# Two margins instead of one in the planner of a hybrid decoder trunk

## The chip, the cores and the metric

The kernel runs on one core of one Trainium2 chip. The metric is the device time of one execution in microseconds (us). Three executions of the kernel before took 1103.56, 1106.44 and 1106.52 us; the median is 1106.44 us.

## The reference

The program is one inference step of a two-layer decoder trunk in fp32 (D_MODEL 2048, a prompt of 256 tokens and 8 sample tokens, so 264 columns). Cut to what matters:

```
h = rms_norm(x, norm_w)
z = h @ w_in                      # 2048 x 7296, columns split among branches
y_a = rwkv_time_mix(z_a, ...)     # 12 heads x 64: decay, delta-rule state scan, group norm, gate
y_b = attention_branch(z_b, ...)  # 3 dilated windows, 12 heads; samples read KV caches of 2048
y_c = pool_branch(z_c, ...)       # causal means over 2, 4, 8, 16 rows, a 128x128 map per group
y = x + concat([y_a, y_b, y_c]) @ w_out   # 2048 x 2048
```

Each layer also returns the updated states and the new K/V rows. The state scan of the prompt is computed in chunks of 64 tokens: triangular systems are inverted by blocks, and four chunks follow one another through small products.

## The kernel before, in words

**The stream.** TensorE's main work is the two large projections, called the stream here. Weights arrive as 512 KB tiles `raw` over SyncE's queue (SP); `stream` (line 323 holds its matmul) splits each into a rounded part `hi` (ScalarE, line 137) and a remainder `lo` (VectorE, line 140) and multiplies hi by the two parts of x and lo by the first part: for one `raw` tile of two 128-column halves, 24 matmuls of 128x128 by 264 columns. Over both layers that are 5472 matmuls against w_in and 1536 against w_out, 7008 in all, into three PSUM banks with the tag `acc`. The order of the column tiles is fixed by the program; w_out takes its rows in quarters in the order 2, 1, 3, 0, so its first matmul needs the attention outputs in the tiles `mb`.

**The side products.** Everything else on TensorE, 2794 instructions, writes the five banks with the tag `a` and is called a side product: transposes (line 118), the rank-64 maps, the blocks of the inversion (`invert`), the chunk products (`chunk`), scores and values of the attention (`b_prompt`), the samples' products over the caches (`b_sample`, with the tiles `vc`, `ex`, `os`), and the pooling maps (`cd`). Some are tied into bundles that stay together. Each reads what ScalarE, VectorE, GpSimd or a transfer has just written, and its result goes back to ScalarE or VectorE. TensorE runs its instructions strictly in the order in which they are written, so a side product whose operand is late holds up the stream matmuls behind it.

**The planner.** The program is first written out branch by branch; then `Plan` puts all instructions of all engines into a new order. `Plan.once` is a list scheduler that simulates the engines with costs per instruction (`cost`, line 1467 on), hop times between engines (`HOP`) and DMA times. An instruction becomes ready when its operands are done in this simulation, plus a hop, plus the instruction's `slack`. Stream matmuls, and instructions that feed them (`hi`, `lo`), have slack 0; all others have `margin`, 350 ns. The slack counts only for operands from another engine or from a transfer:

```
slack = [0 if stream[k] or k in feeds else margin for k in range(n)]
...
r = fin[k] if dma[k] else fin[k] + (100 if eng[q] == "SP" else HOP[e, eng[q]])
if e != eng[q] or dma[k]:
    r += slack[q]
```

On TensorE a ready side product goes before any stream matmul; the stream fills the rest. On the other engines the ready instruction with the longest remaining chain goes first. The plan is made twice: the first pass gives the start times from which non-weight loads are held back (`ahead`, 12000 ns before their first reader). Only the order goes into the kernel (`apply` adds an order between neighbours on each engine and queue). No instruction waits for a clock: on the chip a slack lives on only as the other instructions that the plan put in between.

**Limits on the order.** Tiles are taken from rings (`z` 5, `raw` 3, `hi` 2, `lo` 3, `tmp` 5, PSUM `acc` 3 and `a` 5), and the tiles of `lpool` (attention and pooling) can't be opened before those of `apool` (time mixing, up to the end of `a_chain`) are closed.

Of the kernel before, what the change touches and what calls it, by code (L numbers as in the profile page):

```python
# [103 lines left out]
class Trunk:  # L104
# [1185 lines left out]
    def run(self):  # L1290
        self.setup()
        with self.tc.tile_pool(name="init", bufs=1, reuse_waits="tile") as ip:
            self.ip, self.early, self.xin = ip, [], []
            calm = ip.tile([P, T], F32, name="calm")
            self.nc.vector.memset(calm, 0.0)
            pt = self.ps("a")
            calmr = ip.tile([P, 512], F32R, name="calmr")
            self.nc.vector.memset(calmr.bitcast(F32), 0.0)
            for _ in range(8):
                self.mm(pt[:, :T], calm[:, :P], calm)  # L1300
            pu = self.ps("a")
            for n, outs, rows in ((T, (pt,), (slice(0, P),)), (T, (pt, pu), (slice(0, P),)), (256, (pt,), (slice(0, P),)),
                                  (512, (pu,), (slice(0, P),)), (P, (pt,), (slice(0, P),)), (T, (pt, pu), UROWS)):
                for i in range(5):
                    r = rows[i % len(rows)]
                    self.mm(outs[i % len(outs)][:, :n], calmr[r, :P], calmr[r, :n])
            self.act(ip.tile([P, 1], F32, name="table"), calm[:, 0:1], AF.Tanh)
            self.params(0)
            for c in range(4):
                x = ip.tile([P, 4, T], F32, tag="xin", name=self.nm("xin"), bufs=4)  # L1310
                self.dma(x, self.ins["x_cm"][4 * c:4 * c + 4].rearrange("k p t -> p k t"))
                self.xin.append(x)
                if c < 3:
                    self.early.append(self.load(self.ins["w_in"][0], 23 * P, 2 * P, c))
            self.accs = self.stream(self.ins["w_in"][0], 23 * P, 2, None, None, begin=True)
            self.dma(self.cbase, self.ins["cbase"])
            self.first_scale()
            self.more_params(0)
        for l in range(self.depth):
            self.layer(l)  # L1320
# [15 lines left out]
class Plan:  # L1336
# [200 lines left out]
                tail[q] = max(tail[q], t)  # L1537
        return tail

    def run(self, factor=1, hop=300, margin=200, batch=0, wait=0, switch=0, quiet=0, lead=1, dyn=(), ahead=0):  # L1540

        self.hold = [0.0] * self.n
        args = factor, hop, margin, batch, wait, switch, quiet, lead, dyn
        if ahead:
            self.once(*args)
            for k, i in enumerate(self.ins):
                if self.dma[k] and not self.feeds(k):
                    self.hold[k] = max(0.0, min([self.start[q] for q in self.after_load[k]], default=0.0) - ahead)
        return self.once(*args)
# [1 line left out]
    def feeds(self, k):  # L1551
        return self.tag[self.first_out[k]].startswith("raw") if self.first_out[k] in self.tag else False

    def once(self, factor, hop, margin, batch, wait, switch, quiet, lead, dyn):
        n, eng, preds, dma, dur, stream = self.n, self.eng, self.preds, self.dma, self.dur, self.stream
        spare = {t: d for t, r in self.ring.items() for m, d in dyn if t.split("_" + self.pool[r[0]])[0] == m}
        tail = self.tails(factor, hop, spare)
        head = [k for k in range(n) if stream[k]][lead - 1]
        prio = [k - 3e9 if k < head else -tail[k] for k in range(n)]
        feeds = {q for k in range(n) if stream[k] for q in preds[k]}  # L1560
        slack = [0 if stream[k] or k in feeds else margin for k in range(n)]
        bust = [self.bus(i) if d else 0 for i, d in zip(self.ins, dma)]
        succ = [[] for _ in range(n)]
        count = [0] * n
# [51 lines left out]
        def take(h):  # L1616
            while h:
                p, k = heapq.heappop(h)
                w = blocked(k)
                if w is None:  # L1620
                    return k
                parked[w].append(k)
            return None
# [5 lines left out]
        while done < n:  # L1629
            while pending and pending[0][0] <= now + 1e-9:  # L1630
                _, k = heapq.heappop(pending)
# [8 lines left out]
            for e in free:  # L1640
                if free[e] > now + 1e-9 or (e == "SP" and hw > now + 700):
                    continue
                if e == "PE" and forced is not None:
                    k = forced
                elif e == "PE":
# [3 lines left out]
                    k = None  # L1649
                    if h:  # L1650
                        go = side_on or h[0][0] < -2e9 or now - since >= wait or sum(dur[x[1]] for x in h) >= batch
                        if go:
                            k = take(h)
# [3 lines left out]
                    if k is None:  # L1657
                        k = take(ready["PE"])
                        if k is None and h:
                            k = take(h)  # L1660
# [3 lines left out]
                else:  # L1664
                    k = take(ready[e])
# [134 lines left out]
def build(nc, shapes, depth=DEPTH):  # L1800
    ins = {n: nc.dram_tensor(f"in_{n}", s, F32, kind="ExternalInput").ap() for n, s in shapes.items()}
    outs = {n: nc.dram_tensor(f"out_{n}", s, F32, kind="ExternalOutput").ap() for n, s in _OUTS}
    with tile.TileContext(nc, schedule_with_timeline_sim=True) as tc, ExitStack() as ctx:
        trunk = Trunk(ctx, tc, ins, outs, depth)
        trunk.run()
        plan = Plan(tc, trunk.bundles)
        plan.run(ahead=12000, switch=105, margin=350, hop=180, factor=0.9, lead=25, quiet=60, dyn=[("a", 2)])
        plan.apply()


# [10 lines left out]
```

## Time and profile before

| | |
|---|---|
| median of three executions | 1106.44 us (1103.56 to 1106.52) |
| the profiled execution's own time | 1103.8 us |
| its span, first to last instruction | 1102.0 us |
| TensorE matmuls busy (PE) | 1053.9 us, 96%, 9802 matmuls |
| TensorE weight loads busy (PEld) | 1004.4 us, 91% |
| VectorE busy (DVE) | 857.2 us, 78% |
| ScalarE busy (ACT) | 546.1 us, 50% |
| GpSimd busy (POOL) | 133.6 us, 12% |
| mean share of the 16 DMA engines | 66% |
| mean granted clock of TensorE | 0.982 of 2.4 GHz |

PE is the engine that runs the matmuls, PEld its weight loads, which overlap them. The end of a matmul is modelled in the trace, so neighbours overlap: the distance from start to start is the pace. "Idle before" in a timeline row is the engine's idle time before that instruction, with the instruction or transfer that released it. The granted clock is 1.00 at 2.4 GHz and 0.50 at 1.2 GHz.

### The profile page before, as it was taken

How to read it: one execution, taken by the hardware profiler on the slowest of the kernel's cores; microseconds unless marked ns; L12 is line 12 of the kernel's file. 1: busy time of each engine (PE TensorE's matmuls, PEld its weight loads, DVE VectorE, ACT ScalarE, POOL GpSimd, SP SyncE). 2: the span in 40 equal slices, each digit the busy share in tenths (PEclk: the TensorE clock that was granted, in tenths of full speed). 3: DMA queues.
4: the chain of work that ended last, by engine and by line, in shares of the span. 5: the costliest groups of instructions: out<-in, count | busy, mean ns of one | idle time of the engine just before them, and what ended most of it. 6: DMA issues, size and time to landing. Idle time of an engine off the chain costs nothing.

```text
span 1102.0 us, 24574 instructions
## 1 busy us (share of the span) xinstructions
PE 1053.9 (96%) x9802; PEld 1004.4 (91%) x9802; DVE 857.2 (78%) x1684; ACT 546.1 (50%) x934; POOL 133.6 (12%) x262
## 2 busy tenths in 40 slices
PE   9999998989999998999999999989899998999998
PEld 8999898978999887999999988988899988879998
DVE  7769968979998887666675898768899869886443
ACT  7646433445645554454464563443466553744332
POOL 0004200200022100010010141001001111000000
PEclk9999999989999999999999999989999989999999
DMA  8654578886368855677765446878864568555774
GB/s 275 209 166 135 151 232 234 243 225 208 116 209 256 267 188 174 197 225 223 231 216 169 154 136 207 226 228 212 230 196 138 172 216 307 167 187 187 226 226 151
DMA packets 154683, 223.64 MB, mean 203 GB/s; under 512 B 75984, under 2 KB 109152, under 8 KB 154552
## 3 DMA queue, kind: packets, MB, share of 16 engines
q1 hardware_dynamic: 146456, 195.94, 58.7%
q0 software_dynamic: 8112, 26.12, 7.2%
q8 instruction: 77, 1.26, 0.5%
q14 instruction: 38, 0.31, 0.1%
HBM read 198.55 MB, written 24.03 MB: 202 GB/s over the span
## 4 chain that ended last, share of the span: by engine, by line
PE 58%; DVE 19%; DMA 12%; issue 5%; ACT 4%; SPq 1%; POOL 0%; DVEq 0%; ACTq 0%; POOLq 0%
PE acc L323 50%; DVE lo L140 6%; PE a L115 5%; DMA raw<-in_w_in 5%; PE a L118 2%; ACT hi L137 2%; DVE s L140 1%; DMA qb<-q_dram 1%; DVE z L140 1%; DMA vc<-in_cache_v_w 1%; SPq L155 1%; DVE bk L149 1%; DMA iv<-rb_dram 1%; ACT uv L137 1%; DVE bk L140 1%
## 5 line engine op out<-in xcount | busy, mean ns | idle before, releaser
L137 ACT ACTIVATE hi<-raw 128x1024 fp32r<-128x1024 f32 (+1 forms) x296 | 309.9, 1047 | 385.7 <-PE acc L323 257.6
L323 PE MATMUL acc<-xh,hi 128*128 128x264 f32 x1824 | 477.5, 291 | 4.3 <-ACT hi L137 3.0
L323 PE MATMUL acc<-xl,hi 128*128 128x264 f32 x1824 | 475.4, 291 | 0.2 <-DVE xl L149 0.2
L140 DVE TENSOR_TENSOR lo<-raw,hi 128x1024 fp32r<-128x1024 f32 (+1 forms) x296 | 357.1, 1207 | 137.2 <-ACT hi L137 135.3
L323 PEld LDWEIGHTS acc<-xh,hi 128*128 128x128 f32 x1824 | 348.2, 191 | 8.9 <-ACT hi L137 3.4
L323 PEld LDWEIGHTS acc<-xl,hi 128*128 128x128 f32 x1824 | 348.5, 191 | 6.2 <-issue 4.5
L323 PE MATMUL acc<-xh,lo 128*128 128x264 f32 x1824 | 300.7, 291 | 2.3 <-DVE lo L140 2.1
L323 PEld LDWEIGHTS acc<-xh,lo 128*128 128x128 f32 x1824 | 252.5, 191 | 9.7 <-issue 4.0
L140 DVE TENSOR_TENSOR z<-acc,rstd 128x264 f32<-128x264 f32 (+1 forms) x112 | 52.1, 466 | 25.0 <-PE acc L323 23.6
L323 PE MATMUL acc<-mb,hi 128*128 128x264 f32 x384 | 57.3, 284 | 0.2 <-DVE xs L140 0.2
L323 PEld LDWEIGHTS acc<-mb,hi 128*128 128x128 f32 x384 | 51.0, 188 | 0.5 <-DVE xs L140 0.5
L323 PE MATMUL acc<-mh,hi 128*128 128x264 f32 x192 | 49.3, 284 | 0.0
L323 PE MATMUL acc<-ml,hi 128*128 128x264 f32 x192 | 49.2, 284 | 0.0
L353 POOL COPY zcol<-z 128x9 f32<-128x9 f32 x50 | 19.4, 387 | 207.8 <-DVE z L140 193.9
L323 PEld LDWEIGHTS acc<-ml,hi 128*128 128x128 f32 x192 | 36.1, 188 | 0.0
L323 PEld LDWEIGHTS acc<-mh,hi 128*128 128x128 f32 x192 | 36.1, 188 | 0.0
L323 PE MATMUL acc<-mb,lo 128*128 128x264 f32 x192 | 33.8, 285 | 0.0
L323 PE MATMUL acc<-mc,hi 128*128 128x264 f32 x256 | 33.6, 284 | 0.0
L323 PE MATMUL acc<-mh,lo 128*128 128x264 f32 x192 | 33.6, 283 | 0.0
L140 DVE TENSOR_TENSOR xs<-acc,res 128x264 f32<-128x264 f32 x32 | 13.9, 433 | 24.3 <-DMA res<-resid 16.6
L323 PEld LDWEIGHTS acc<-mc,hi 128*128 128x128 f32 x256 | 32.1, 188 | 0.0
L323 PEld LDWEIGHTS acc<-mh,lo 128*128 128x128 f32 x192 | 27.6, 188 | 0.0
(357 smaller groups left out, 1309.7 us busy)
## 6 DMA issues: line engine op xcount, KB each, us to landing
raw<-in_w_in SPq DMA_DIRECT2D x224, 512.0 KB
raw<-in_w_out SPq DMA_DIRECT2D x64, 512.0 KB
g_dram<-gs SPq DMA_DIRECT2D x8, 768.0 KB
gs<-g_dram SPq DMA_DIRECT2D x8, 768.0 KB
kc<-in_cache_k_w POOLq DMA_DIRECT2D x12, 512.0 KB, 7.2
qb<-q_dram SPq DMA_DIRECT2D x12, 512.0 KB
vc<-in_cache_v_w POOLq DMA_DIRECT2D x12, 512.0 KB, 5.0
s<-in_state_wkv POOLq DMA_DIRECT2D x12, 256.0 KB, 5.0
```

The costliest lines, as they stand in the source:

```text
L115: self.note(self.nc.tensor.matmul(out, lhsT, rhs, start=start, stop=stop))
L118: self.note(self.nc.tensor.transpose(out, in_, self.c("ident")[base:base + k, base:base + k]))
L137: self.nc.scalar.activation(out, in_, func, **kw)
L140: self.nc.vector.tensor_tensor(out, a, b, op=op)
L149: self.nc.vector.scalar_tensor_tensor(out, a, s, b, op0=op0, op1=op1)
L155: self.nc.sync.dma_start(out, in_)
L323: self.nc.tensor.matmul(accs[t][:, :T], a[:, k4, cs], b[k], start=first, stop=q == order[3] and k4 == 3 and late == 1)
L353: self.nc.gpsimd.tensor_copy(self.zcol[:, :, a], z[:, NP - 1:T])
```

## The change

`run` and `once` take a second margin, `care`. Side products on TensorE get `care` as their slack, all other instructions that had `margin` keep it. The call sets `care` to 1200 ns and lowers `margin` from 350 to 200 ns. Nothing else changes: the same instructions are emitted, in another order.

```diff
-    def run(self, factor=1, hop=300, margin=200, batch=0, wait=0, switch=0, quiet=0, lead=1, dyn=(), ahead=0):
+    def run(self, factor=1, hop=300, margin=200, batch=0, wait=0, switch=0, quiet=0, lead=1, dyn=(), ahead=0, care=350):
...
-        args = factor, hop, margin, batch, wait, switch, quiet, lead, dyn
+        args = factor, hop, margin, batch, wait, switch, quiet, lead, dyn, care
...
-    def once(self, factor, hop, margin, batch, wait, switch, quiet, lead, dyn):
+    def once(self, factor, hop, margin, batch, wait, switch, quiet, lead, dyn, care):
...
-        slack = [0 if stream[k] or k in feeds else margin for k in range(n)]
+        slack = [0 if stream[k] or k in feeds else care if eng[k] == "PE" else margin for k in range(n)]
...
-        plan.run(ahead=12000, switch=105, margin=350, hop=180, factor=0.9, lead=25, quiet=60, dyn=[("a", 2)])
+        plan.run(ahead=12000, care=1200, switch=105, margin=200, hop=180, factor=0.9, lead=25, quiet=60, dyn=[("a", 2)])
```

## Rows read from the trace of the kernel before

**Rows 1.** The page's part 1: busy us (share of the span) xinstructions.

```profile
PE 1053.9 (96%) x9802; PEld 1004.4 (91%) x9802; DVE 857.2 (78%) x1684; ACT 546.1 (50%) x934; POOL 133.6 (12%) x262
```

**Rows 2.** Windows: engines' busy us (x instructions), PEclk, DMA share, GB/s.

```profile
80.00:140.00 60.00, 56.93 (x483) 53.71 (x482) 56.22 (x120) 32.82 (x61) 19.61 (x38) 1.00 0.50 154
260.00:320.00 60.00, 58.06 (x654) 55.81 (x650) 58.45 (x144) 34.75 (x59) 8.49 (x14) 1.00 0.61 183
...
433.20:551.20 118.00, 118.00 (x974) 118.00 (x973) 76.43 (x111) 57.88 (x82) 8.12 (x15) 1.00 0.68 214
```

**Rows 3.** TensorE's waits, whole span: us in total, times, longest us.

```profile
PE a L115 <- issue: 5.1, 3, 2.6
PE a L115 <- DMA vc<-in_cache_v_w: 3.4, 2, 1.9
PE acc L323 <- ACT hi L137: 3.0, 2, 1.8
...
PE a L115 <- DVE calm L1295: 1.2, 1, 1.2
...
PE a L115 <- ACT bt L137: 0.3, 1, 0.3
```

**Rows 4.** TensorE's timeline: side products with idle time before them.

```profile
96.21 0.39 PE L115 MATMUL a<-aux,up 128*128 128x264 f32 x1 [0.21 <-ACT u L137]
...
361.11 0.71 PE L118 MATMUL a<-cbase,p 128*128 128x128 f32 x2 [0.70 <-ACT p L137]
...
421.73 0.44 PE L118 MATMUL a<-cbase,os 128*128 128x128 f32 x2 [1.73 <-ACT os L137]
...
427.50 0.64 PE L115 MATMUL a<-vc,ppad 128*32 128x256 f32 x8 [1.89 <-DMA vc<-in_cache_v_w]
...
888.67 0.48 PE L115 MATMUL a<-qkt,qkt 64*128 64x128 f32 x2 [1.76 <-ACT pt L137]
...
980.87 0.64 PE L115 MATMUL a<-vc,ppad 128*32 128x256 f32 x8 [1.52 <-DMA vc<-in_cache_v_w]
```

**Rows 5.** Span and mean granted clock of the core.

```profile
core 0: 1102.0 us, clock 0.982
```

**Rows 6.** Windows of 20 us around two stalls, columns as in rows 2.

```profile
360.00:380.00 20.00, 19.19 (x140) 16.54 (x139) 16.62 (x34) 11.96 (x33) 2.72 (x5) 0.91 0.89 289
...
880.00:900.00 20.00, 17.32 (x119) 16.54 (x118) 14.32 (x38) 10.71 (x25) 3.67 (x8) 0.83 0.66 206
```

**Rows 7.** TensorE's timeline around 405 us: lone side products between stream matmuls.

```profile
405.16 0.28 PE L323 MATMUL acc<-xh,hi 128*128 128x264 f32 x1
405.37 0.26 PE L118 MATMUL a<-cbase,ssm 48*128 48x48 f32 x1
405.56 0.39 PE L323 MATMUL acc<-xl,hi 128*128 128x264 f32 x1
```

**Rows 8.** VectorE's timeline: the last attention outputs of each layer.

```profile
439.71 0.77 DVE L140 TENSOR_TENSOR mb<-sgb,mb 128x264 fp32r<-128x264 f32 x2
...
988.77 0.77 DVE L140 TENSOR_TENSOR mb<-sgb,mb 128x264 fp32r<-128x264 f32 x2
```

**Rows 9.** TensorE's timeline: the first matmuls of w_out in each layer.

```profile
458.05 1.13 PE L323 MATMUL acc<-mb,hi 128*128 128x264 f32 x8
...
1004.77 1.13 PE L323 MATMUL acc<-mb,hi 128*128 128x264 f32 x8
```

**Rows 10.** ScalarE's timeline ahead of the stall at 888 us.

```profile
887.29 1.06 ACT L137 ACTIVATE hi<-raw 128x1024 fp32r<-128x1024 f32 x1 [2.92 <-DMA raw<-in_w_in]
888.25 0.36 ACT L137 ACTIVATE pt<-a 128x256 f32<-128x256 f32 x1
```

**Rows 11.** The page's part 5: the stream's largest group, mean ns of one.

```profile
L323 PE MATMUL acc<-xh,hi 128*128 128x264 f32 x1824 | 477.5, 291 | 4.3 <-ACT hi L137 3.0
```

## The prediction

> **What bounds the kernel now.** I read the page's busy shares first: TensorE is busy 1053.9 of 1102.0 us, every other engine far less [rows 1]. So the time is TensorE's work plus 48.1 us in which it stood. Next the windows, for the pace of undisturbed work: from 433.2 to 551.2 us, inside the first w_out, 974 matmuls take 118 us, 121 ns each, without a gap [rows 2]. The 7008 stream matmuls at that pace are 849 us, and no order changes that; 253 us are left for 2794 side products, changes between the two kinds, standing time and slow clock.
>
> Then the table of TensorE's waits, for what the 48.1 us are. It explains 44: 6.8 us before stream matmuls (the largest is 3.0 for `hi`), 1.2 at the start (`calm`), and 36.1 before side products. Of the last, 5.1 have no releaser ("issue"); 31.0 us are 36 stalls in which a side product stood at the head of TensorE's queue with its operand not there [rows 3]. The timeline gives each its place: the first is 0.21 us at 96.21, the last 1.52 us at 980.87; 18 of the 36 exceed 0.85 us [rows 4]. Behind each stand stream matmuls whose weights were mostly there. Last the clock: its mean is 0.982, so 1102.0 x 0.018 = 19.8 us of full speed were not granted, in stretches at 1.2 GHz that follow such stalls; the window from 360 to 380 us, which holds the 0.70 us stall at 361.11, has 0.91, that from 880 to 900 us, after 1.76 us, 0.83 [rows 4 to 6].
>
> **The change, part by part.**
>
> *Side products later (care 1200 for 350).* No instruction is added. The order puts up to 850 ns more of other TensorE work between an operand's planned end and its product, some 7 stream matmuls of 121 ns. An operand late by more than 350 ns costs a stall now; afterwards the same lateness costs at most 850 ns less. Per stall the gain is the smaller of its length and 0.85 us. Over all 36: 18 x 0.85 = 15.3, plus 8.0 for the shorter ones, 23.3 us. That is the upper end.
>
> Two deductions. First, 17 stalls (9.5 us, capped 8.7) lie between 80 and 140, 260 and 320, 620 and 680, and 800 and 860 us. There VectorE is busy 56.2 and 58.5 of 60 us; layer 1 repeats both to 0.2 us [rows 2]. When the engine that makes the operands is full, its lateness is a matter of throughput: pushing the product back moves the stall, and the `lo` and `z` of the stream come from the same VectorE. I count these as nothing; the other end is 8.7. Second, of the other 19 (capped 14.6), five pairs lie less than 6 us apart, as 421.73 and 427.50 [rows 4]. If the first product's delay also gives the second's producer its time, a pair was one lag and gains 0.85 once: 14.6 - 5 x 0.85 = 10.3. I take 10.3, since the members of such pairs mostly hang on one chain (`os` after `vc`); ends 0 and 23.3.
>
> *Clock.* Where a stall disappears altogether, its stretch at 1.2 GHz can too. The 0.70 us at 361.11 is under 0.85, and its window lacks 20 x 0.09 = 1.8 us; the one at 888.67 is halved, and I take half of that window's 20 x 0.17 = 3.4 us [rows 4, 6]. Together 3.5 us; ends 0 and 19.8. The longer stalls, transfers and "issue", keep theirs.
>
> *Other engines earlier (margin 200 for 350).* Evacuations, VectorE steps and the DMA issues on SP and POOL are planned 150 ns nearer to their operands. When one waits on the chip, what is queued behind it on its engine waits: the `hi` and `lo` of the stream above all. ScalarE is half idle [rows 1] and hides most of it; VectorE in the four full stretches doesn't. It stood there 2 x 3.8 + 2 x 1.5 = 10.6 us [rows 2]; at worst that doubles. Ends 0 (none new) and 10.6; I take 2, nearer to nothing, because TensorE waited only 6.8 us for the stream's own operands in the whole span [rows 3]. A gain has a reason too: shorter hops on every chain.
>
> *More changes between stream and side products.* Products formerly ready together may now stand apart. A lone 48x48 transposition takes the stream from 405.16 to 405.56, 0.40 us instead of 0.12 [rows 7]; 0.28 at most per split run. I take seven such splits, 2 us; ends -2 (runs merge) and 6 (twenty splits).
>
> *Loads.* A load held back to 12 us before its reader moves with the reader, and its issue on SP or POOL too; nothing waits for it, as reader and load move together. Priced at nothing; without that cover it is another stall like the 1.89 us for `vc` [rows 4].
>
> *Sum.* -10.3 - 3.5 + 2 + 2 = -9.8 us. The profiled execution took 1103.8 us (span 1102.0 and 1.8 around it), giving 1094. The median of the runs shown is 1106.44, 0.24% above it; I add half of that, 1.3: **1095 us**.
>
> **A rule weighed.** TensorE's row says 48.1 us idle, the weight loads' row 97.6 [rows 1]. The Trainium skill (Perfetto Trace Analysis, Identifying the Most-Contended Engine) says that the matmul share is no good measure of TensorE's headroom and names the weight loads' busy share instead. By that rule the gain of 10.3 scales to 10.3 x 97.6 / 48.1 = 20.9 and the time comes to about 1084; by the stalls' rows it is 1095. This trace agrees that the matmul row hides something (a matmul is drawn 291 ns long at a pace of 121).
>
> **The rivals.**
>
> *Hidden stalls go too (about 1083).* A stream matmul is drawn 291 ns long but follows its neighbour after 121 [rows 2, 11]; a wait of up to 170 ns disappears beneath the one before. The 36 stalls would be longer by 36 x 0.17 = 6.1 us, and as many again too short to see would add 6.1. The gain is 12 more, 1095 - 12. Against it: a shown stall over 0.85 us gains nothing from being longer still.
>
> *The lag is throughput everywhere (about 1106).* Not only VectorE's full stretches: the stall at 888.67 waits for `pt`, which ScalarE ran only after a `hi` that had waited 2.92 us for its weights [rows 4, 10]. A product placed later then stands behind stream matmuls that want the same weights, so TensorE stands as long and the waits carry stream names. Only the five stalls under 0.85 us that the first deduction leaves, from 0.36 to 0.73 and 2.7 us together, go, and the costs of 4 eat them: 1103.8 + 1.3 + 1.3. Here the change does not do what it says. For it: VectorE's 95% in the full stretches. Against it: most other stalls name a single late step while the stream has its operands.
>
> *The chains outlast the stream (about 1112, slower).* Products later means chains longer. On the path through `invert` and four chunks I count 16 steps into TensorE and about 20 into other engines: 16 x 0.85 - 20 x 0.15 = +10.6 us before `apool` closes and the attention may start. On the samples' attention, five transpositions and two products for each of three groups, 11 x 0.85 - 20 x 0.15 = +6.4. Sum +17.0. The last `mb` is written at 440.5 and 989.5, w_out starts at 458.05 and 1004.77: slack 17.6 and 15.2 us [rows 8, 9]. It decides at the point where `mb` ends later than the last w_in matmul. By this count it just about holds, costing at most 1.8 us in layer 1. If the shorter hops give nothing back, because those steps wait for their engines anyway, the growth is 27 x 0.85 = 23.0 us; TensorE stands empty for 5.4 and 7.8 us ahead of w_out, and after each it runs a stretch at 1.2 GHz, 1.8 us as in the window of 361: 16.8 us on top of the forecast, 1111.8. Against it: the order delays a product only where stream work stands in front, and that work is not lost.
>
> **How the numbers follow.** Forecast 0.47, hidden stalls 0.10, throughput 0.20, chains 0.20; 0.03 is left for anything else. The range reaches from below the hidden-stall case, 1080, to just past the chains, 1113. About 0.3% (3.3 us) is what a measurement can tell from no change: faster is under 1103.1, slower over 1109.8. Faster: 0.42 of the forecast's 0.47, 0.10, and 0.05 of the throughput case, 0.57. Same: 0.05 and 0.15, with 0.02 of the chains, 0.22. Slower: 0.18 of the chains and 0.03, 0.21. The forecast's own range is 1086 to 1102.
>
> **What would show it.** TensorE's waits before side products fall from 36 stalls and 31.0 us to about 20 us, those over 0.85 us first; waits before stream matmuls stay near 6.8. The granted clock rises from 0.982 to about 0.985, the 361 us window to 1.00. The four full VectorE stretches keep their stalls. The attention's last `mb` comes later against the first w_out matmul, with slack left over. It is wrong if the stalls keep their sum under other names (throughput), if TensorE has a gap just ahead of w_out (chains), or if TensorE's busy time, not its idle time, makes the difference (splits, hidden waits).

## The result and the profile after

The changed kernel takes 1098.93 us (median of 18 runs, 1090.11 to 1102.34) against 1104.80 for the kernel before, timed beside it (1096.75 to 1108.23). The ratio is 0.9943, with a 95% interval of 0.9922 to 0.9965: faster by 0.6% where 1.0% was forecast. The profiled execution has a span of 1097.6 us, 4.4 less than before.

The page's part 1 of the kernel after, and below it the span and mean granted clock [rows 1, 5].

```profile
PE 1055.8 (96%) x9802; PEld 1005.7 (92%) x9802; DVE 857.0 (78%) x1684; ACT 546.8 (50%) x934; POOL 132.1 (12%) x262
```

```profile
core 0: 1097.6 us, clock 0.984
```

TensorE's idle time (span less busy) fell from 48.1 to 41.8 us, by 6.3. Its busy time *rose* by 1.9 us although the instructions are the same. The clock not granted is 1097.6 x 0.016 = 17.6 us, 2.2 less.

TensorE's waits of the kernel after, whole span: us in total, times, longest us [rows 3].

```profile
PE a L115 <- issue: 5.0, 3, 2.0
PE acc L323 <- DVE lo L140: 4.0, 4, 2.1
PE acc L323 <- ACT hi L137: 3.3, 3, 1.6
PE a L118 <- DVE compb L140: 2.8, 1, 2.8
PE a L115 <- DVE uv L701: 2.7, 2, 2.4
PE a L115 <- DMA vc<-in_cache_v_w: 2.7, 2, 1.5
...
PE a L118 <- DVE z L140: 0.2, 1, 0.2
```

Over the whole table, leaving out "issue" and the start, stalls before side products are 32 with 22.3 us, where there were 36 with 31.0; those over 0.85 us are 7, where there were 18. Waits before stream matmuls are 8.4 us, where there were 6.8. Two entries of the same table for the kernel before:

```profile
PE a L118 <- ACT os L137: 2.7, 2, 1.7
PE a L118 <- DVE z L140: 2.6, 3, 1.2
```

Waits for `os` fell from 2.7 to 0.3 us. Waits for `z` fell from 2.6 to 0.2, but the transpositions of `z` did not gain: whatever the table names as their releaser, they held TensorE 3.6 us before and 3.4 now (sums over the timeline), 2.84 of it in one stall that `compb` ended. That stall and one of 2.44 us that `uv` ended are the longest now.

TensorE's timeline of the kernel after. The first, third, fourth and last line are the products of 361.11, 421.73, 427.50 and 980.87 us [rows 4]; idle time before them in brackets.

```profile
360.35 0.71 PE L118 MATMUL a<-cbase,p 128*128 128x128 f32 x2 [0.29 <-ACT p L137]
...
196.68 0.69 PE L118 MATMUL a<-cbase,z 128*128 128x128 f32 x2 [2.84 <-DVE compb L140]
...
409.36 0.44 PE L118 MATMUL a<-cbase,os 128*128 128x128 f32 x2 [0.28 <-ACT os L137]
...
414.51 0.64 PE L115 MATMUL a<-vc,ppad 128*32 128x256 f32 x8 [1.15 <-DMA vc<-in_cache_v_w]
...
793.47 0.33 PE L115 MATMUL a<-uv,bt 128*64 128x64 f32 x2 [2.44 <-DVE uv L701]
...
972.13 0.64 PE L115 MATMUL a<-vc,ppad 128*32 128x256 f32 x8 [1.53 <-DMA vc<-in_cache_v_w]
```

The old stalls shrank by 0.41 (0.70 to 0.29), 1.45 and 0.74 us, and the last did not move. That is the direction that a margin gives, but not its size: the second lost more than the 0.85 us of the cap. A new order moves the producers too. The two new long ones have one kind of cause, which VectorE's timeline of the kernel after shows:

```profile
193.71 0.69 DVE L140 TENSOR_TENSOR s<-s,svec 128x512 f32<-128x512 f32 x1 [5.32 <-DMA sval<-sv_dram]
194.31 1.22 DVE L140 TENSOR_TENSOR lo<-raw,hi 128x1024 fp32r<-128x1024 f32 x1
...
196.05 0.57 DVE L140 TENSOR_TENSOR z<-acc,rstd 128x256 f32<-128x256 f32 x1
196.47 0.17 DVE L140 TENSOR_TENSOR compb<-acc,rstd 128x8 f32<-128x8 f32 x1
...
791.66 0.69 DVE L140 TENSOR_TENSOR s<-s,svec 128x512 f32<-128x512 f32 x1 [4.45 <-DMA s<-in_state_wkv]
792.27 0.68 DVE L152 TENSOR_REDUCE asa<-s 128x8 f32<-128x512 f32 x1
792.87 1.13 DVE L701 COPY uv<-a 64x384 f32<-64x384 f32 x2
```

VectorE stood 5.32 and 4.45 us at a step of the samples' state update whose loads (`sval`, `s`) had not landed. `lo`, `z` and `uv` were queued behind that step, and the transposition at 196.68 and the chunk product at 793.47 behind them. In the kernel before VectorE's waits of the state update `s` for transfers add up to 2.4 us (its longest entry stands below), here to 11.0.

```profile
DVE s L140 <- DMA svec<-sk_dram: 2.2, 2, 1.1
```

The full VectorE stretches of the kernel after, and the windows around 361 and 888 us (columns as in [rows 2, 6]).

```profile
80.00:140.00 60.00, 58.52 (x491) 55.01 (x490) 57.07 (x121) 33.30 (x61) 17.99 (x37) 1.00 0.50 158
260.00:320.00 60.00, 58.06 (x707) 55.23 (x707) 57.19 (x151) 34.02 (x60) 7.95 (x17) 1.00 0.58 176
...
360.00:380.00 20.00, 19.49 (x155) 17.74 (x154) 19.21 (x41) 12.20 (x32) 4.58 (x8) 1.00 0.74 241
880.00:900.00 20.00, 18.20 (x141) 17.04 (x141) 16.86 (x28) 10.82 (x19) 4.24 (x6) 0.91 0.89 293
```

From 80 to 140 us TensorE is busy 1.6 us more than before, and VectorE 0.85. The 361 us window is at full clock; the other went from 0.83 to 0.91. What is left at 1.2 GHz there follows another wait, of 1.44 us for a `hi` of the stream at 882.59.

Last the attention against w_out: VectorE's last `mb`, then TensorE's first w_out matmuls, of the kernel after [rows 8, 9].

```profile
435.41 0.77 DVE L140 TENSOR_TENSOR mb<-sgb,mb 128x264 fp32r<-128x264 f32 x2
...
981.75 0.77 DVE L140 TENSOR_TENSOR mb<-sgb,mb 128x264 fp32r<-128x264 f32 x2
```

```profile
453.86 1.13 PE L323 MATMUL acc<-mb,hi 128*128 128x264 f32 x8
...
1000.20 1.13 PE L323 MATMUL acc<-mb,hi 128*128 128x264 f32 x8
```

The slack is 17.7 us in both layers (17.6 and 15.2 before). Against the stream the chains did not grow; they ended 4.3 and 7.0 us earlier, and w_out began 4.2 and 4.6 us earlier.

### The profile page after: what moved, and what is told of

Same layout as the page of the kernel before. It is cut to its first block, busy times and chain, and to the rows that moved or that the text cites. A ratio compares the mean times of both kernels' runs of the same rounds, so it can differ in the third digit from the quotient of the medians.

```text
span 1097.6 us, 24559 instructions
## 1 busy us (share of the span) xinstructions
PE 1055.8 (96%) x9802; PEld 1005.7 (92%) x9802; DVE 857.0 (78%) x1684; ACT 546.8 (50%) x934; POOL 132.1 (12%) x262
## 4 chain that ended last, share of the span: by engine, by line
PE 52%; DVE 21%; DMA 14%; ACT 6%; issue 6%; SPq 2%; DVEq 0%; ACTq 0%; POOLq 0%
PE acc L323 45%; DVE lo L140 7%; PE a L115 5%; DMA raw<-in_w_in 5%; DMA qb<-q_dram 3%; ACT hi L137 2%; PE a L118 2%; SPq L155 2%; DVE s L140 1%; DVE z L140 1%; DMA rwkv_a_up<-in_rwkv_a_up 1%; DMA vc<-in_cache_v_w 1%; DVE bk L149 1%; DVE tm L140 1%; DMA g_dram<-gs 1%
## 5 line engine op out<-in xcount | busy, mean ns | idle before, releaser
L323 PE MATMUL acc<-xh,lo 128*128 128x264 f32 x1824 | 297.6, 290 | 4.0 <-DVE lo L140 4.0
L323 PEld LDWEIGHTS acc<-mb,hi 128*128 128x128 f32 x384 | 50.9, 188 | 0.3
L140 DVE TENSOR_TENSOR s<-s,svec 128x512 f32<-128x512 f32 x36 | 24.6, 684 | 10.9 <-DMA sval<-sv_dram 5.3
```

Of the source, the lines that this page charges most:

```text
L140: self.nc.vector.tensor_tensor(out, a, b, op=op)
L323: self.nc.tensor.matmul(accs[t][:, :T], a[:, k4, cs], b[k], start=first, stop=q == order[3] and k4 == 3 and late == 1)
```

## The experiments

The theory was that lateness is capped: a later place for the side products removes their stalls, and the smaller margin of the others matters little. The rivals were that the smaller margin brings the gain (shorter hops), and that every order is just another draw. All kernels differ from the changed one in the numbers of one line, unless a diff says more. Each is given below with its ratio to the kernel before, timed beside it.

**Each half alone, and two other doses**

```diff
-        plan.run(ahead=12000, care=1200, switch=105, margin=200, ...
+        plan.run(ahead=12000, care=1200, switch=105, margin=350, ...   # care1200_m350
+        plan.run(ahead=12000, care=350, switch=105, margin=200, ...    # care350_m200
+        plan.run(ahead=12000, care=2400, switch=105, margin=200, ...   # care2400_m200
+        plan.run(ahead=12000, care=0, switch=105, margin=350, ...      # care0_m350
```

*Care alone.* 

> Care 1200 alone; the other engines keep 350 ns. Theory 'later products' (the gain is capped lateness of the operands of side products): TensorE's stalls before side products fall to 20 to 24 us as in the change (22.3, from 31.0), ratio to the kernel before 0.993 to 0.997. Rival 'shorter hops' (the gain comes from margin 200): stalls may fall, but the ratio is 0.998 to 1.003. Rival 'another draw' (any new order scatters by half a per cent): no relation between stalls and time.

Measured: 1082.85 us, ratio 0.9811 (0.9783 to 0.9839), far more than any theory had. Stalls before side products are 15.4 us in 21 places, where 20 to 24 us were expected. Its page and its clock:

```profile
PE 1043.0 (97%) x9802; PEld 995.3 (92%) x9802; DVE 858.1 (79%) x1684; ACT 547.5 (51%) x934; POOL 131.9 (12%) x262
```

```profile
core 0: 1079.9 us, clock 0.994
```

The profiled span is 17.7 us below the changed kernel's: 4.9 of that is idle time (36.9 against 41.8), 12.8 is *busy* time. Between these two profiles the clock accounts for 11.1: 1079.9 x 0.006 = 6.5 us not granted, against 17.6. But the changed kernel's profile was an execution with little clock, 0.984; its 18 executions were granted 0.983 to 0.992 and lack 13.9 us on average, the six of this kernel 7.0. So over all executions the clock has 6.9 of the 14.0 us between the mean spans (1095.9 and 1082.0), about half. "Shorter hops" is refuted: the order without them is the faster one.

*Margin alone.* 

> Margin 200 alone; side products keep 350 ns. 'Later products': stalls before side products 30 to 36 us, ratio 1.000 to 1.004. 'Shorter hops': ratio 0.993 to 0.997 with stalls near 31 us. 'Another draw': anything within half a per cent.

Measured: ratio 0.9969 (0.9950 to 0.9989), stalls 29.1 us. Against the stalls the smaller margin does almost nothing, nearly as expected (30 to 36); the 0.3% it gained was not expected, and no more than what care 0 gained.

*Twice the care.* 

> Twice the care of the change. 'Later products' by caps: another 1200 ns leaves of the 22.3 us the parts over 1.2 us, some 5 to 14 us of stalls, and unless the chains outlast the stream the ratio to before is 0.988 to 0.993; the last mb would stand under 10 us ahead of the first w_out matmul (18.4 and about 17 in the change). If the chains decide, there is a gap of TensorE ahead of w_out and the ratio is over 0.995. 'Another draw': stalls still about 22 us.

Measured: ratio 0.9870 (0.9842 to 0.9899), stalls 15.0 us in 20 places, waits before the stream 12.9. The expected 5 to 14 us was too low by a little. VectorE's last `mb` and TensorE's first w_out matmul in layer 0, then in layer 1:

```profile
441.07 0.77 DVE L140 TENSOR_TENSOR mb<-sgb,mb 128x264 fp32r<-128x264 f32 x2
986.27 0.78 DVE L140 TENSOR_TENSOR mb<-sgb,mb 128x264 fp32r<-128x264 f32 x2
```

```profile
459.27 1.13 PE L323 MATMUL acc<-mb,hi 128*128 128x264 f32 x8
986.54 1.13 PE L323 MATMUL acc<-mb,hi 128*128 128x264 f32 x8
```

In layer 0 the slack is still 17.4 us. In layer 1 it is used up: w_out begins while the last `mb` are being written, and TensorE has no gap there. The `mb` came 5.7 and 4.5 us later than in the change, so the chains did grow, but by far less than the rival's count (27 steps of 1.2 us). Most of the slack in layer 1 went because the stream got to w_out 13.7 us sooner. So the point that the slower rival named is reached at 2400 in one layer, and not at 1200; what more care would cost was not run.

*No care.* 

> Side products with no care at all (0 for 350 ns), the others as before: the dose in the other direction. 'Later products': the 36 stalls grow by up to 0.35 us each and short ones appear, 40 to 48 us of stalls before side products, ratio 1.006 to 1.012. 'Shorter hops' and 'another draw': 0.995 to 1.005 with stalls near 31 us.

Measured: ratio 0.9965 (0.9940 to 0.9990), stalls 30.7 us, where 40 to 48 were expected. The dose below 350 has no effect that can be seen; 12.5 us of waits without a releaser ("issue", 5.1 before) may hide some of it. The capped-lateness theory misses here.

**Neighbours, 100 ns to each side**

```diff
-        plan.run(ahead=12000, care=1200, switch=105, margin=200, ...
+        plan.run(ahead=12000, care=1100, switch=105, margin=350, ...   # care1100_m350
+        plan.run(ahead=12000, care=1300, switch=105, margin=350, ...   # care1300_m350
+        plan.run(ahead=12000, care=1100, switch=105, margin=200, ...   # care1100_m200
+        plan.run(ahead=12000, care=1300, switch=105, margin=200, ...   # care1300_m200
```

> A neighbour of care 1200 with margin 350 (0.981 of before). Theory 'margin 200 costs' (the other engines' smaller margin loses about 1.3%): ratio 0.978 to 0.985, like its neighbour. Rival 'another draw' (each order is a draw, and which stalls end in a slow stretch of the clock is chance): ratio anywhere between 0.978 and 0.996. Both: stalls before side products 14 to 20 us.

> The neighbour on the other side. 'Margin 200 costs': 0.978 to 0.985. 'Another draw': 0.978 to 0.996. Stalls before side products 14 to 18 us.

> A neighbour of the change (0.994) with margin 200. 'Margin 200 costs': 0.990 to 0.997, stalls before side products 20 to 25 us, and the clock at 1.2 GHz for 30 us or more. 'Another draw': 0.980 to 0.997.

> The neighbour of the change on the other side. 'Margin 200 costs': 0.988 to 0.996, stalls 18 to 23 us. 'Another draw': 0.980 to 0.997; one of the two margin 200 neighbours under 0.987 would speak for it.

Measured: 0.9832 (0.9808 to 0.9856) and 0.9825 (0.9798 to 0.9852) with margin 350, stalls 13.4 and 14.5 us; 0.9836 (0.9811 to 0.9860) and 0.9914 (0.9882 to 0.9945) with margin 200, stalls 23.2 and 25.7 us. The three orders with margin 350 agree to about 0.2%. With margin 200, 100 ns of care move the time by 1.1%, so the changed kernel is in part an unlucky draw. At care 1100 the smaller margin cost nothing (0.9836 against 0.9832), outside what "margin 200 costs" expected and the sign that was named for "another draw"; at 1300 it cost 0.9%. The stalls were 22 to 26 us in all three orders with margin 200 and 13 to 15 in all with 350, which seemed to make a rule.

**Is it the margin, and whose?**

```diff
-        plan.run(ahead=12000, care=1200, switch=105, margin=200, ...
+        plan.run(ahead=12000, care=1200, switch=105, margin=500, ...   # care1200_m500
+        plan.run(ahead=12000, care=700, switch=105, margin=350, ...    # care700_m350
```

```diff
-        slack = [0 if stream[k] or k in feeds else care if eng[k] == "PE" else margin for k in range(n)]
+        slack = [0 if stream[k] or k in feeds else care if eng[k] == "PE" else 350 if eng[k] in ("DVE", "ACT") else margin for k in range(n)]   # care1200_m200_queues
```

> Margin 500 for the other engines, care 1200. Theory 'small margins make the operands late' (stalls before side products were 22 to 26 us in three orders with margin 200 and care 1100 to 1300, 13 to 15 us in three with margin 350): stalls fall again or hold, 9 to 15 us, ratio 0.976 to 0.985. Rival 'margins only lengthen chains': stalls hold at 13 to 15 us, and the attention comes out too late for w_out, ratio over 0.988. Rival 'another draw': stalls anywhere from 13 to 26 us.

Measured: 0.9838 (0.9799 to 0.9876), but stalls of 21.8 us in 30 places. The rule "small margins make the operands late" falls: a larger margin brought them back. The time held all the same, with 10.8 us of clock not granted.

> A middle dose of care, margin 350 as before. 'Capped lateness': of the 31.0 us of stalls in the kernel before, the smaller of each and 0.35 us goes, 11 us: 18 to 22 us are left, ratio 0.988 to 0.994. 'Another draw': 0.982 to 1.000 with no relation to the stalls.

Measured: 0.9943 (0.9917 to 0.9970), stalls 22.5 us in 39 places; both are just past the edge of what was expected (18 to 22 us, 0.988 to 0.994). Waits before the stream rose to 14.5 us, so the idle time stayed at 48.5 us.

> The change with margin 200 only for the instructions of SP and POOL (DMA issues and GpSimd's copies); VectorE and ScalarE keep 350 ns. If the computing engines' margin makes the operands late: stalls before side products 13 to 17 us as with 350 for all, ratio 0.979 to 0.986. If the loads' does: 21 to 26 us, ratio 0.989 to 0.996, the stalls naming transfers or what follows them.

Measured: 0.9868 (0.9829 to 0.9908), a time as with 350 for all or nearly, stalls of 23.5 us as with 200. It answers neither way, but it shows the clock. Its page and clock:

```profile
PE 1043.9 (96%) x9802; PEld 996.1 (92%) x9802; DVE 856.0 (79%) x1684; ACT 548.6 (50%) x934; POOL 134.4 (12%) x262
```

```profile
core 0: 1086.5 us, clock 0.994
```

It stands as long as the changed kernel (1086.5 - 1043.9 = 42.6 us idle against 41.8) with as much stalling (23.5 against 22.3), and is 11.1 us shorter: its clock lacks 6.5 us, the changed kernel's 17.6. Between these two profiles that is the whole difference; over all executions (9.1 us on average against 13.9) it is 4.8 of the 8.4 us between the mean spans. TensorE's timeline of this kernel at its longest stall:

```profile
200.66 0.44 PE L118 MATMUL a<-cbase,z 128*128 128x128 f32 x2 [3.50 <-DVE z L140]
...
201.06 0.29 PE L323 MATMUL acc<-xl,hi 128*128 128x264 f32 x1
201.19 0.29 PE L323 MATMUL acc<-xh,hi 128*128 128x264 f32 x1
```

A transposition of `z` near the same time in the kernel after, also behind a late load of the state update:

```profile
196.68 0.69 PE L118 MATMUL a<-cbase,z 128*128 128x128 f32 x2 [2.84 <-DVE compb L140]
...
198.05 0.42 PE L323 MATMUL acc<-xh,hi 128*128 128x264 f32 x1
198.27 0.42 PE L323 MATMUL acc<-xl,hi 128*128 128x264 f32 x1
```

After 3.50 us the stream runs on at 0.13 us from start to start, at 2.4 GHz (the granted clock from 200 to 206 us is 1.00); after 2.84 us it runs at 0.22, at 1.2 GHz.

**The changed kernel once more**

> The changed kernel itself, profiled and timed once more. If the stretches at 1.2 GHz are drawn anew in each execution: the stalls before side products stay at 22 to 24 us in the same places, but the slow stretches (34 us in the first profile, mean clock 0.984) lie elsewhere or are fewer, 14 to 34 us, and the clock is 0.985 to 0.993; the ratio over more runs is 0.990 to 0.994. If the order decides them: the same places at 197, 227, 234, 739, 773, 794, 882, 920 and 951 us within 2 us, clock 0.983 to 0.985, ratio 0.993 to 0.996.

Measured: 0.9931 (0.9901 to 0.9961), the same result. The profiled execution:

```profile
core 0: 1091.1 us, clock 0.987
```

```profile
PE 1051.8 (96%) x9802; PEld 1002.7 (92%) x9802; DVE 857.0 (79%) x1684; ACT 547.1 (50%) x934; POOL 133.4 (12%) x262
```

Stalls are 23.4 us in 29 places; the span is 6.5 us shorter than in the first profile, 2.5 in idle time and 4.0 in busy time. Windows of the first profile, then of this one, around three of the slow places (columns as in [rows 2]):

```profile
186.00:206.00 20.00, 17.16 (x130) 16.95 (x129) 13.53 (x22) 7.67 (x9) 1.13 (x2) 0.91 0.67 207
728.00:748.00 20.00, 17.90 (x135) 17.69 (x134) 16.97 (x26) 8.49 (x11) 1.06 (x3) 0.91 0.57 183
780.00:800.00 20.00, 17.30 (x177) 16.61 (x178) 14.20 (x23) 7.07 (x11) 2.10 (x4) 0.91 0.72 209
```

```profile
186.00:206.00 20.00, 17.80 (x134) 17.60 (x133) 14.17 (x23) 8.30 (x9) 1.51 (x3) 0.91 0.65 208
728.00:748.00 20.00, 19.38 (x160) 19.17 (x159) 18.51 (x28) 9.90 (x12) 1.94 (x3) 1.00 0.57 179
780.00:800.00 20.00, 19.62 (x240) 18.56 (x239) 17.16 (x28) 8.67 (x12) 2.94 (x5) 1.00 0.83 230
```

The first recurs with its stall; at the other two the second execution had neither the long stall nor the slow stretch. Of the nine places that were expected if the order decided alone, two returned within 2 us (197 and 227). But layer 1 runs 1 to 10 us earlier in the second execution, and by their place in the program two more returned: the product behind the wait for `cm` (919.68, then 911.22 us) and a run of small products `al`, 4 rows each (950.09, then 940.14). At the others the slow stretch stayed away, once behind a longer wait: 1.44 us for `hi` at 882.59 in the first execution was followed by 1.2 GHz, 2.52 us for it at 876.37 in the second by full clock.

The `al` place shows one thing more. Windows ahead of it and behind it, of the first execution, then of the second:

```profile
940.00:950.00 10.00, 10.00 (x80) 8.63 (x78) 6.98 (x22) 6.92 (x21) 0.00 (x0) 1.00 0.35 108
950.00:955.00 5.00, 5.00 (x35) 3.76 (x35) 3.56 (x7) 0.21 (x1) 0.00 (x0) 0.66 0.32 105
```

```profile
930.00:940.00 10.00, 10.00 (x80) 8.63 (x79) 6.93 (x22) 6.97 (x21) 0.00 (x0) 1.00 0.34 108
940.00:945.00 5.00, 5.00 (x36) 3.91 (x35) 3.60 (x7) 0.21 (x1) 0.00 (x0) 0.66 0.33 105
```

TensorE is shown busy throughout, and the clock falls all the same, in both executions. So not every slow stretch follows a stall. The order sets where TensorE may stand or run small products; the single execution decides how long it stands, and at most places whether the clock falls.

**All orders side by side.** Idle is span less busy. Lost clock is span x (1 - clock). The rest is what remains of the span when both are taken away. Stalls are the waits before side products, "issue" and the start left out. All but the ratio are of the one profiled execution; the last column is the lost clock averaged over all executions of the kernel, their number in brackets.

| kernel | ratio | stalls | idle | lost clock | rest | lost clock, mean |
|---|---|---|---|---|---|---|
| before | 1 | 31.0 | 48.1 | 19.8 | 1034.1 | 16.2 (65) |
| care 0, margin 350 | 0.9965 | 30.7 | 50.9 | 17.6 | 1034.4 | 17.2 (12) |
| care 350, margin 200 | 0.9969 | 29.1 | 46.7 | 17.6 | 1037.4 | 16.3 (12) |
| care 700, margin 350 | 0.9943 | 22.5 | 48.5 | 15.4 | 1037.3 | 13.3 (12) |
| **after** (1200, 200) | 0.9943 | 22.3 | 41.8 | 17.6 | 1038.2 | 13.9 (18) |
| after, second profile | 0.9931 | 23.4 | 39.3 | 14.2 | 1037.6 | 12.5 (9) |
| care 1100, margin 200 | 0.9836 | 23.2 | 40.7 | 8.7 | 1037.2 | 7.8 (5) |
| care 1300, margin 200 | 0.9914 | 25.7 | 40.7 | 8.7 | 1041.6 | 9.3 (6) |
| 1200, 200 for SP and POOL only | 0.9868 | 23.5 | 42.6 | 6.5 | 1037.4 | 9.1 (6) |
| care 2400, margin 200 | 0.9870 | 15.0 | 37.2 | 10.8 | 1036.1 | 6.9 (6) |
| care 1100, margin 350 | 0.9832 | 13.4 | 39.0 | 11.9 | 1034.7 | 10.0 (5) |
| care 1200, margin 350 | 0.9811 | 15.4 | 36.9 | 6.5 | 1036.5 | 7.0 (6) |
| care 1300, margin 350 | 0.9825 | 14.5 | 40.1 | 13.1 | 1035.1 | 9.1 (5) |
| care 1200, margin 500 | 0.9838 | 21.8 | 35.5 | 10.8 | 1036.5 | 9.9 (6) |

The rest stays within 1034 to 1042 us for every order: it is the work. What an order can change is idle time and clock, 68 us before, 59 after, 43 in the best. With care from 0 to 700, they come to 64 to 69; with 1100 and more, to 43 to 54, but for the first profile of the changed kernel. That care shortens the time is shown by nine orders with 1100 or more, all faster than before by 0.6 to 1.9%, against 0.3 to 0.6% for the three with 700 or less. Idle time parts the two groups cleanly (at most 42.6 us, at least 46.7); the time does so but for the changed kernel, which ties with care 700, and which also lost more clock than the other eight, on average over its executions too. "Another draw" explains the spread within the groups, not the step between them. The stalls alone do not order the times: with 21.8 to 25.7 us of them the ratio was anything from 0.9836 to 0.9943. The best version is care 1200 with margin 350, faster than both kernels.

## Why the prediction was right, and where its sizes were off

**The direction and the mechanism held.** Stalls before side products were to fall from 31.0 to about 20 us, those over 0.85 us first, and fell to 22.3 (23.4 in the second profile), those over 0.85 us from 18 to 7. Care alone brings it; margin 200 alone left 29.1.

**The closeness of the number is partly luck.** Care alone was priced at -10.3 and -3.5 with +2 for splits, -11.8 us or 1.1%, and measured 1.9% faster. Margin 200 was priced at +2 us, 0.2%; alone it measured 0.3% faster, but beside care 1200 it cost 1.3% (0.9943 against 0.9811), some 15 us. Care was priced too low and margin 200 beside it far too low, and the two nearly cancelled. The neighbours of the change, at 1085.37 and 1093.51 us, show that much of that cost belongs to this one order. All orders that were run, 1082.85 to 1101.43 us, lie inside the stated range, so the range tells little.

**Side products later (-10.3 us).** The stalls outside the four full VectorE stretches gave not 10.3 but 4.8 us (from 21.4 to 16.5 in the timeline), and the stretches that were counted as nothing gave 3.6 (from 9.5 to 5.9). Those 3.6 came from two of the four: from 80 to 140 us the stalls fell from 3.1 to 1.3 us and from 620 to 680 from 3.0 to 1.4, while from 260 to 320 and from 800 to 860 they kept 1.9 and 1.3 of 1.9 and 1.5, as forecast. "Throughput" was the wrong word for the first two: from 80 to 140 us VectorE had 0.85 us more to give, and stalls there were lateness like the others. Outside, new stalls of 2.84 and 2.44 us took back half of what the old ones gave. The cap itself, the smaller of a stall's length and the added margin, is borne out only roughly. Care 700 came near it (8.5 us less where 11 were counted) and care alone, 15.6 us less, lies between its ends; but care 0 added no stalls, care 1200 with margin 500 left 21.8 us where margin 350 left 15.4, and the pair at 421.73 and 427.50, which was to gain 0.85 once, gained 2.19.

**Other engines earlier (2 us).** Waits before the stream rose by the 1.6 us (6.8 to 8.4) that this step looked for, but the larger damage stood elsewhere than it looked: VectorE's waits for the state update's loads, 2.4 to 11.0 us, came out as side-product stalls. That the smaller margin makes these loads late was not shown: over the other orders such waits vary from 0.4 to 13.6 us with no relation to margin. Whether the holding back of loads (`ahead`) does it was not run.

**The clock (-3.5 us).** It moved 2.2 us in this profile and 5.6 in the next, and 2.8 on average over all executions (16.2 to 13.4, the change's 27 taken together), so for the change the size held. The two windows that were named gave 1.8 and 1.6 us (0.91 to 1.00, 0.83 to 0.91), as forecast, the second in part by luck: what is left there hangs on another wait. What failed is the step's picture, in which slow stretches go place by place with their stalls and no others come: new places replaced old ones, and one place has no stall. For care alone the term was too small, 9.2 us on average (16.2 to 7.0).

**More changes between the two kinds (2 us).** The rest of the table rose by 4.1 us, from 1034.1 to 1038.2 (the clock's last digit leaves half a microsecond open in each). What it consists of stays open: busy time that is neither clock nor instruction count, with short waits beneath the drawn ends of matmuls and costs of changing as candidates. No run separated the two.

**The rivals.** *Hidden stalls* would have shown as falling busy time; after the clock's share it rose. *Throughput everywhere* is refuted by nine orders whose stalls and idle time fell. *Chains outlast the stream* did not happen at 1200, slack 17.7 us; at 2400 the slack of layer 1 is gone, which is the point the rival named. The sign of its growth was wrong at 1200: the chains ended earlier. A likely reason, not shown, is that a product that doesn't stall TensorE lets the whole chain come earlier. The weight loads' idle time, by which the gain was scaled to about 1084 us, was no better guide: it fell by 5.7 us (97.6 to 91.9), the matmuls' by 6.3, and the time came to 1098.93.

Between the two profiles the span fell by 4.4 us where the sum had 9.8: -8.7 of stalls for -10.3, +1.6 in the stream for +2, -2.2 of clock for -3.5, +4.1 of rest for +2, and +0.8 of "issue" and small waits in no table. The medians fell by 5.9 us (1104.80 to 1098.93).

## What to carry to other kernels

Where an in-order engine takes both streaming work and work that depends on others, plan the dependent work later than the model says it is ready; the lateness of real operands is then paid with filler work, and the chains need not suffer. Judge such a margin by several neighbouring values, because a new order is also a new draw (1.1% here for 100 ns), and separate idle time from lost clock before comparing. Change one margin at a time: here the half that looked harmless took away two thirds of the gain at care 1200 and nothing at 1100, so how much of that is the margin's and how much this order's stays open. And read the clock from several executions: two single profiles put 11.1 us between the change and care 1200 with margin 350 down to it, the averages 6.9.

## What the runs showed that was not expected

One stall of 3.50 us was followed by the stream at 2.4 GHz, and one of 2.84 us by 1.2 GHz; at one place the clock fell in both executions behind small products, with TensorE shown busy. Two executions of the same program granted 0.984 and 0.987, and differed by 6.5 us in span. In single profiles with 22 to 24 us of stalls the clock not granted varied from 6.5 to 17.6 us, and averaged over executions it runs from 6.9 to 17.2 over the orders, 0.9% of the time. Where and how long TensorE stands, and what it runs, weighs in it beside how much it stands in all.
